# Two GELUs and three half projections at the end of attention, in a transformer layer on one core

## The chip, the cores and the metric

The kernel runs on one core of a Trainium2 chip. The metric is the device time of one execution in microseconds, as the median of several runs. Lower is better. The core has TensorE (PE, matrix products and transposes), VectorE (DVE), ScalarE (ACT), GpSimd (POOL) and SyncE (SP, which issues the transfers). Each engine takes its own instructions in order and waits on semaphores for the others.

## The reference

One layer with two groups of heads. All inputs are float32, the sequence has 2048 frames, the model width is 1024.

```python
h = rmsnorm(x, norm_mix_g)
proj = h @ w_in
y_ssm = s5_mixer(proj[..., :512], ...)          # scan, then gelu, then GLU:
#   y = gelu(y);  y = y * sigmoid(y @ w_glu + b_glu)
y_att = chunked_attention(q, k, v, rel_bias)    # softmax over 9 chunks of 64 frames
mixed = concat([rmsnorm(y_ssm, norm_ssm_out_g), rmsnorm(y_att, norm_att_out_g)])
x = x + mixed @ w_out
h2 = rmsnorm(x, norm_ffn_g)
x = x + (silu(h2 @ w_gate) * (h2 @ w_up)) @ w_down
return rmsnorm(x, norm_final_g)
```

## The kernel before

Products are made in float32 halves: an operand is cast to a high part (`gh`, `woh`, `pth`; line 153 or 884, ScalarE) and VectorE takes the rest (`gl`, `wol`, `ptl`; line 153 or 885); `mm3` then issues three products for one. Time is cut into four blocks of 512 frames (`sb`).

The program runs in stages: the input projection, attention together with the state-space scan, the mixing stage (`mix_phase`), gate and up, down. Attention goes in 128 steps, each of 128 queries of one head: `scores(s)`, then two steps later `transp(s - 2)`, which transposes the probabilities on PE into `pt` (one buffer) and casts them to `pth` and `ptl`, and after each fourth step `pv_head`, the product with the values (`pj`). Every step `s` also advances the other units. From step 119 on one of these units is the first part of the mixing stage: `mix_phase` is a generator of which `MIX_N` pieces are taken within attention, spread over steps 122 to 129, and the rest behind it.

The pieces are: fetch `yr` (the scan's output for blocks 0 and 1, four transfers) and the gate weights (`load_wg`, through the two buffers `sg`); the GELU of block 0 (`load(0, True)`, line 1050) and its casts `gh`, `gl`; the gate products of block 0 (`glu`, sixteen groups of three products into `pf`); the GELU of block 1 (`load(1, True)`). Behind attention come the gate products of block 1 (into `big`, four buffers), the split of the output weights `w_out` (`split_wo`), and the output projection. In `glu` with `late=True` the sums go back into `yr` (line 1077), and one sigmoid for all four (line 1079) and four products (line 1081) follow.

The output projection `w_out(sb, b, i)` makes two of eight row groups (a pair) in one `big` buffer. It is a generator with two halves: 24 products with the attention operands, then 24 with those of the state-space group. In block 0 two pairs are held: the first half of pair 0 is issued, then the spread of the second norm's factor `no` over partitions (four transposes `big<-ident,no`, `spread`), then the scaling `rstd2` and the cast `mixed(b, 1)` of the state-space operands, then the first half of pair 1.

The scheduler reorders ScalarE, VectorE and SP by its own estimate of readiness; the PE order is pinned to the order of the code (`keep_in_program_order`). A table of functions is loaded on ScalarE (`ACT_TABLE_LOAD`) whenever the next function is not in the one that is loaded; exponential, GELU and sigmoid are in different ones here.

Of the kernel before, what the change touches and what calls it, by code (L numbers as in the profile page):

```python
# [93 lines left out]
def f32(ap):  # L94
    return ap.bitcast(F32)
# [24 lines left out]
def spread(k, te, pb, o, c):  # L120

    for i in range(4):
        te.transpose(pb[:, i * P : (i + 1) * P], o[:, c + i : c + i + 1].to_broadcast([P, P]), k.ident[:])
# [21 lines left out]
def mm3(te, out, whi, wlo, xhi, xlo, first, last, **kw):  # L145
    te.matmul(out, whi, xhi, start=first, stop=False, **kw)
    te.matmul(out, whi, xlo, start=False, stop=False, **kw)
    te.matmul(out, wlo, xhi, start=False, stop=last, **kw)


def split(k, hi, lo, raw):
    nc = k.nc
    return nc.scalar.copy(hi, raw), nc.vector.tensor_tensor(lo, raw, f32(hi), op=ALU.subtract)  # L153
# [533 lines left out]
def att_phase(k, ident, S, aw, x0, roots):  # L687

    tc, nc, io, pfs = k.tc, k.nc, k.io, k.pfs
    with ExitStack() as cx:  # L690
# [181 lines left out]
        def transp(st):  # L872
            sb, pr, hh, qp = st
            hd = st_head[sb, 2 * pr + hh]
            if qp == 0:
                hd.p = k.t(aa, "pth", [P, 5, 4, P], F32R), k.t(aa, "ptl", [P, 5, 4, P], F32R)
            pth, ptl = hd.p
            s, k0 = hd.s.pop(qp)
            pt = k.t(psum, "pt", [P, 5, P], bufs=1)
            for kb in range(k0, qp + 5):  # L880
                k.ta.transpose(pt[:, kb % 5, :], s[:, (kb - k0) * P : (kb - k0 + 1) * P], ident[:])
            runs = [(0, 5)] if sb else ([(4, 5)] if qp == 0 else [(4, 5), (0, qp)])
            for a, b in runs:
                nc.scalar.copy(pth[:, a:b, qp, :], pt[:, a:b, :])  # L884
                nc.vector.tensor_tensor(ptl[:, a:b, qp, :], pt[:, a:b, :], f32(pth[:, a:b, qp, :]), op=ALU.subtract)  # L885

        def pv_head(st):
# [72 lines left out]
        for s in range(N + LAG + 2):  # L960
            if s == OPEN:
                aw.release()
                mix = mix_phase(k, S, lambda: k.t(pfs, "pf", [P, 512]))
                units += [Unit(islice(mix, MIX_N), MIX_N, GSTART, N + LAG, GSTART - OPEN)]
            if s == GSTART:
# [13 lines left out]
        yield mix  # L979


PY, PZ = 8, 1
MIX_N = 17 + PY + PZ


def mix_phase(k, S, bank):

    tc, nc, io = k.tc, k.nc, k.io
    te = k.te
    with ExitStack() as cx:  # L990
# [44 lines left out]
        def fetch(sb):  # L1035
            yrs[0] = k.t(my, "yr", [P, 4, L, 128])
            for f in range(4):
                nc.sync.dma_start(yrs[0][:, f], S["y"][:, f * P : (f + 1) * P, sb * 64 : sb * 64 + 128].rearrange("j p t -> p j t"))

        def load(sb, one=False):  # L1040
            b = B()
            b.o = {}
            yt = k.t(my, "ys", [P, 4, SB], bufs=2)
            b.ys, b.g = [yt[:, f] for f in range(4)], []
            if sb and sb % 2 == 0:
                fetch(sb)
            yv = b.yr = yrs[0][:, :, :, (sb % 2) * 64 : (sb % 2 + 1) * 64]
            fs = [slice(0, 4)] if one else [slice(f, f + 1) for f in range(4)]
            for s in fs:
                nc.scalar.activation(yt[:, s].rearrange("p f (c j) -> p f c j", j=L), yv[:, s].rearrange("p f j c -> p f c j"), AF.Gelu_apprx_tanh)  # L1050
            for f in range(4):
                gh, gl = k.t(my, f"gh{f}", [P, SB], F32R), k.t(my, f"gl{f}", [P, SB], F32R)
                split(k, gh[:], gl[:], b.ys[f])
                b.g.append((gh, gl))
            return b

        def load_a(b, sb):
            b.ya = [k.t(mw, f"ya{f}", [P, SB])[:] for f in range(4)]
            for f in range(4):
                nc.sync.dma_start(b.ya[f], S["ya"][sb, f * P : (f + 1) * P])  # L1060
            b.sqa = squares(b.ya)
# [33 lines left out]
        def rstd2(b, c, pb):  # L1095

            for f, (y, g) in enumerate(zip((b.ya, b.ys)[c], (ga, gs)[c : c + 1] * 4)):
                nc.vector.scalar_tensor_tensor(y, y, g[:, f : f + 1], pb, op0=ALU.mult, op1=ALU.mult)

        def big():  # L1100
            return k.t(psum, *BIG)
# [10 lines left out]
        def mixed(b, c):  # L1112
            for n, (q, y) in enumerate(zip(QS[4 * c : 4 * c + 4], (b.ya, b.ys)[c])):
                mt = k.t(mx, f"m{q}", [P, 2, SB], F32R)
                mh, ml = b.m[q] = mt[:, 0], mt[:, 1]
                split(k, mh, ml, y)

        def w_out(sb, b, i):
            ts = slice(sb * SB, (sb + 1) * SB)
            if i == 0:  # L1120
                b.sa = k.t(k.mf, "sa", [P, SB], bufs=2)
            rows = slice(i * P, (i + 2) * P)
            xt = k.t(wr, "xt", [P, 1024], bufs=2)
            xv = xt[:].rearrange("p (q t) -> p q t", q=2)
            nc.sync.dma_start(xv, io["xt"][rows, ts].rearrange("(q p) t -> p q t", p=P))
            ps = k.t(psum, *BIG)
            for n, c in ((n, c) for m in range(2) for c in range(2) for n in range(4 * m, 4 * m + 4)):
                if n == 4 and c == 0:
                    yield
                fc = slice((i + c) * P, (i + c + 1) * P)  # L1130
                for q in QS[n : n + 1]:
                    mm3(te, ps[:, c * 512 : (c + 1) * 512], W[q][0][:, fc], W[q][1][:, fc], b.m[q][0], b.m[q][1], n == 0, n == 7)
            nc.vector.tensor_tensor(xt[:], xt[:], ps[:], op=ALU.add)
            nc.sync.dma_start(S["x1"][rows, ts].rearrange("(q p) t -> p q t", p=P), xv)
            if i == 0:
                nc.scalar.activation(b.sa[:], xt[:, :512], AF.Square)
                nc.scalar.activation(xt[:, 512:], xt[:, 512:], AF.Square)
            else:
                nc.scalar.activation(xt[:], xt[:], AF.Square)
                nc.vector.tensor_tensor(b.sa[:], b.sa[:], xt[:, :512], op=ALU.add)  # L1140
            nc.vector.tensor_tensor(b.sa[:], b.sa[:], xt[:, 512:], op=ALU.add)
            yield

        def next_block(sb):
            b = load(sb)
            load_a(b, sb)
            for _ in glu(b, big):
                pass
            return b
# [12 lines left out]
        yield  # L1162
        mw = rx.enter_context(tc.tile_pool(name="mw", reuse_waits="tile", bufs=2, side="right"))
        wr = rx.enter_context(tc.tile_pool(name="wr", reuse_waits="tile", bufs=2, side="right"))
        b = load(0, True)
        load_a(b, 0)
        raws = [load_wo(n, wr, "xt") for n in range(2)]
        for _ in range(PY):
# [1 line left out]
        for n, _ in enumerate(glu(b, bank, True)):  # L1170
# [4 lines left out]
                spread(k, te, pb, b.o[0], 0)  # L1175
                rstd2(b, 0, pb[:])
            yield
        nxt = load(1, True)
        for _ in range(PZ):
            yield  # L1180

        def bk():
            nonlocal psum
# [14 lines left out]
        for sb in range(NSB):  # L1198
            if sb:
                b.m = {}  # L1200
                mixed(b, 0)
            if sb == 0:
                held = [w_out(0, b, 2 * n) for n in range(2)]
                next(held[0])
                ps = big()
                spread(k, te, ps[:, :512], b.o[1], 0)
                with tc.high_priority():
                    rstd2(b, 1, ps[:, :512])
                    mixed(b, 1)
                next(held[1])  # L1210
            else:
                mixed(b, 1)
            for n in range(4):
                if n == 0 and 0 < sb < NSB - 1:
                    nxt = next_block(sb + 1)
                if sb or n > 1:
                    for _ in w_out(sb, b, 2 * n):
                        pass
                else:
                    next(held[n])  # L1220
                if n in (0, 1) and xr:
                    next(xr)
                if n in (1, 2) and sb + 1 < NSB:
                    norm(nxt, n - 1)
                for _ in range(PRE0.get((sb, n), 0)):
                    next(pre)
                if (sb, n) == (NSB - 1, 1):
                    rx.close()
                    k.ga1 = tc.alloc_tile_pool(name="ga1", reuse_waits="tile", bufs=1, side="right")
                    k.gr = tc.alloc_tile_pool(name="gr", reuse_waits="tile", bufs=2, side="right")  # L1230
                    wr = cx.enter_context(tc.tile_pool(name="wr2", reuse_waits="tile", bufs=2, side="right"))
                    k.hT = build(k, S, 0, k.ga1, EARLY)
            if sb < NSB - 1:
                xr = rstd_steps(k, te, psum, k.mf, BIG, b.sa[:], D, S["rsn"][:, sb * SB : (sb + 1) * SB])
            if sb == 1:
                pre = pre_steps(k, S, 0, pre_tiles().__next__, True)
            k.last = b.sa[:]
            b = nxt
# [498 lines left out]
```

## Time and profile before

| | us |
|---|---|
| median of 3 runs | 2264.51 |
| lowest, highest | 2261.2, 2265.51 |
| profiled execution, its own time | 2267.91 |
| its span, first to last instruction | 2266.1 |
| PE busy | 2165.6 (96%) |
| VectorE busy | 1542.4 (68%) |
| ScalarE busy | 1003.3 (44%) |
| granted TensorE clock, mean | 0.982 |

Times in the views are microseconds from the start of the span. A bracket behind a row gives the idle time of the engine ahead of it and the instruction that ended it. The stretch that the change touches lies between 664 and 790, where attention ends and the mixing stage begins.

### The profile page before, as it was taken

Reading aid. Unit: us, or ns where it says so; the run is one execution under the profiler, and the core shown is the slowest. Engines: PE = TensorE matmul, PEld = TensorE weight load, DVE = VectorE, ACT = ScalarE, POOL = GpSimd, SP = SyncE. Lnnn points to the kernel's source line nnn. Section 1 sums busy time; section 2 is a strip of 40 time slices with the busy share of each in tenths; the row PEclk is TensorE's granted clock in tenths of the full one; section 3 lists DMA queues with packets and bytes.
Section 4 is the critical chain, followed back from the end, with each engine's and each line's share of the span. In section 5 each row is a group of like instructions: output and inputs, shape, how many; then the busy total and the mean of one; then the engine's idle time right before and its main releaser. Section 6 shows DMA issues by size and latency. Waiting matters only on the chain.

```text
span 2266.1 us, 30134 instructions
## 1 busy us (share of the span) xinstructions
PE 2165.6 (96%) x10632; PEld 1825.8 (81%) x10632; DVE 1542.4 (68%) x2695; ACT 1003.3 (44%) x1656; POOL 351.2 (15%) x827
## 2 busy tenths in 40 slices
PE   8988899999997899999999999999999999999997
PEld 6777788898986788778888887888888778888886
DVE  7756666556557756776766668766656477688776
ACT  5445555556557442353333335333333443353322
POOL 2246576656500000000000000000000010000000
PEclk9999999999998899999999999999999999999999
DMA  8878876666552435754556457645433395465652
GB/s 276 254 244 261 268 233 207 192 190 205 187 168 100 138 109 188 251 168 144 180 176 209 162 198 269 199 163 190 140 97 112 102 385 182 167 227 181 216 183 75
DMA packets 194903, 430.41 MB, mean 190 GB/s; under 512 B 19904, under 2 KB 38384, under 8 KB 187648
## 3 DMA queue, kind: packets, MB, share of 16 engines
q1 hardware_dynamic: 187104, 403.58, 53.8%
q0 software_dynamic: 7648, 24.92, 3.6%
q8 instruction: 83, 1.36, 0.2%
q14 instruction: 68, 0.56, 0.1%
HBM read 288.95 MB, written 131.10 MB: 185 GB/s over the span
## 4 chain that ended last, share of the span: by engine, by line
PE 78%; DMA 7%; DVE 6%; ACT 3%; issue 2%; SPq 0%; DVEq 0%; ACTq 0%
PE X L76 20%; PE ps L76 17%; PE Y L76 10%; PE pf L76 10%; PE big L76 6%; PE W L76 5%; PE pj L76 4%; PE pt L79 2%; PE sc L76 2%; DMA acc<-x 2%; DMA lo<-hc 1%; DMA xt<-in_xt 1%; DVE lo L153 1%; DMA hc<-gh 1%; DVE ptl L885 1%
## 5 line engine op out<-in xcount | busy, mean ns | idle before, releaser
L76 PE MATMUL X<-hi,c 128*128 128x512 f32 x1408 | 450.8, 391 | 7.4 <-DVE c L153 5.1
L76 PE MATMUL ps<-hd,hd 128*128 128x512 f32 (+1 forms) x1968 | 429.6, 380 | 3.0 <-DVE hd L153 2.0
L76 PEld LDWEIGHTS ps<-hd,hd 128*128 128x128 f32 x1968 | 357.5, 189 | 73.6 <-DVE hd L153 2.7
L76 PEld LDWEIGHTS X<-hi,c 128*128 128x128 f32 x1408 | 265.1, 188 | 64.1 <-DVE c L153 6.0
L76 PE MATMUL X<-lo,c 128*128 128x512 f32 x704 | 274.6, 390 | 0.0
L153 ACT CAST hd<-hd 128x1536 fp32r<-128x1536 f32 (+1 forms) x106 | 147.5, 1394 | 232.5 <-DMA hd<-hq 170.9
L76 PE MATMUL Y<-hi,c 128*128 128x512 f32 x704 | 226.0, 392 | 3.8 <-DVE c L153 2.3
L153 DVE TENSOR_TENSOR hd<-hd 128x1536 fp32r<-128x1536 f32 (+1 forms) x106 | 174.1, 1644 | 36.2 <-ACT hd L153 35.8
L153 DVE TENSOR_TENSOR c<-S,c 128x512 fp32r<-128x512 f32 x176 | 121.0, 688 | 103.6 <-ACT c L153 103.3
L1516 POOL DMA_DIRECT2D hd<-hq x7 | 5.3, 755 | 1173.2 <-PE X L76 1161.5
L1408 ACT COPY u<-X 128x512 f32<-128x512 f32 x132 | 77.4, 587 | 199.9 <-PE X L76 199.9
L153 ACT CAST c<-S 128x512 fp32r<-128x512 f32 x176 | 109.5, 622 | 122.5 <-PE Y L76 63.8
L76 PE MATMUL big<-m,woh 128*128 128x512 f32 x512 | 162.6, 399 | 0.0
L76 PEld LDWEIGHTS Y<-hi,c 128*128 128x128 f32 x704 | 133.3, 189 | 32.4 <-DVE c L153 2.8
L1550 DVE TENSOR_TENSOR acc<-acc,ps 128x512 f32<-128x512 f32 x196 | 130.2, 682 | 41.6 <-PE ps L76 41.3
L76 PEld LDWEIGHTS X<-lo,c 128*128 128x128 f32 x704 | 132.6, 188 | 27.4
L76 PE MATMUL pf<-hi,w 128*128 128x512 f32 x416 | 149.1, 410 | 0.0
L153 ACT CAST c<-raw 128x512 fp32r<-128x512 f32 x132 | 82.2, 622 | 149.1 <-PE Y L76 69.1
L76 PE MATMUL Y<-lo,c 128*128 128x512 f32 x352 | 137.7, 391 | 0.0
L885 DVE TENSOR_TENSOR ptl<-pt,pth 128x640 fp32r<-128x640 f32 (+3 forms) x152 | 98.3, 647 | 56.1 <-ACT pth L884 54.7
L869 ACT ACTIVATE s<-s,mn 128x640 f32<-128x640 f32 (+4 forms) x128 | 98.0, 765 | 64.1 <-DVE mn L866 58.1
L884 ACT CAST pth<-pt 128x640 fp32r<-128x640 f32 (+3 forms) x152 | 83.8, 551 | 85.6 <-PE pt L79 80.9
(448 smaller groups left out, 4274.1 us busy)
## 6 DMA issues: line engine op xcount, KB each, us to landing
w<-wss SPq DMA_DIRECT2D x36, 1024.0 KB, 6.2
hq<-g SPq DMA_DIRECT2D x140, 256.0 KB, 2.1
hd<-hq SPq DMA_DIRECT2D x35, 768.0 KB, 4.4
hd<-wc SPq DMA_DIRECT2D x35, 768.0 KB, 6.0
raw<-in_w_gate SPq DMA_DIRECT2D x44, 512.0 KB, 3.7
raw<-in_w_up SPq DMA_DIRECT2D x44, 512.0 KB, 4.2
wc<-px SPq DMA_DIRECT2D x66, 256.0 KB, 3.1
wss<-w SPq DMA_DIRECT2D x12, 1024.0 KB, 6.5
```

The source lines that it names most:

```text
L76: return self.tc.keep_in_program_order(self.tc.nc.tensor.matmul(*a, **b))
L79: return self.tc.keep_in_program_order(self.tc.nc.tensor.transpose(*a, **b))
L153: return nc.scalar.copy(hi, raw), nc.vector.tensor_tensor(lo, raw, f32(hi), op=ALU.subtract)
L869: nc.scalar.activation(s[:, :nk], s[:, :nk], AF.Exp, bias=mn[:], scale=-1.0, accum_out=sums[sb, pr][:, hh, qp : qp + 1])
L884: nc.scalar.copy(pth[:, a:b, qp, :], pt[:, a:b, :])
L885: nc.vector.tensor_tensor(ptl[:, a:b, qp, :], pt[:, a:b, :], f32(pth[:, a:b, qp, :]), op=ALU.subtract)
L1408: nc.scalar.copy(u[:], ps[:])
L1516: (nc.gpsimd if aside else nc.sync).dma_start(f32(lo), src.rearrange("g p c -> p g c"))
L1550: V.tensor_tensor(a, a, ps[:], op=ALU.add)
```

## The change

Four things are edited. `transp` keeps its last cast `pth` in `k.pth`. `load` makes the GELU in one piece only for block 1, and there `issue_after` queues it behind the last cast of probabilities; for all other blocks, block 0 among them, it is made in four pieces. One piece of `mix_phase` that only let time pass (`PZ`) is gone, so 25 pieces instead of 26 are spread over the last steps. And three pairs of the output projection are held instead of two, with the first halves of two of them ahead of the spread and that of the third behind it.

```diff
             for a, b in runs:
-                nc.scalar.copy(pth[:, a:b, qp, :], pt[:, a:b, :])
+                k.pth = nc.scalar.copy(pth[:, a:b, qp, :], pt[:, a:b, :]).ins
...
-PY, PZ = 8, 1
-MIX_N = 17 + PY + PZ
+PY = 8
+MIX_N = 17 + PY
...
-        def load(sb, one=False):
+        def load(sb):
...
-            fs = [slice(0, 4)] if one else [slice(f, f + 1) for f in range(4)]
-            for s in fs:
+            def gelu(s):
                 nc.scalar.activation(yt[:, s].rearrange("p f (c j) -> p f c j", j=L), yv[:, s].rearrange("p f j c -> p f c j"), AF.Gelu_apprx_tanh)
+
+            if sb == 1:
+                with tc.issue_after(k.pth):
+                    gelu(slice(0, 4))
+            else:
+                for f in range(4):
+                    gelu(slice(f, f + 1))
...
-        b = load(0, True)
+        b = load(0)
...
-        nxt = load(1, True)
-        for _ in range(PZ):
-            yield
+        nxt = load(1)
...
             if sb == 0:
-                held = [w_out(0, b, 2 * n) for n in range(2)]
+                held = [w_out(0, b, 2 * n) for n in range(3)]
                 next(held[0])
+                next(held[1])
                 ps = big()
                 spread(k, te, ps[:, :512], b.o[1], 0)
                 with tc.high_priority():
                     rstd2(b, 1, ps[:, :512])
                     mixed(b, 1)
-                next(held[1])
+                next(held[2])
...
-                if sb or n > 1:
+                if sb or n > 2:
                     for _ in w_out(sb, b, 2 * n):
```

Beside the edits the scheduler moves ScalarE's instructions. ScalarE before, at the first GELU (`ys_8026`): the cast of step 119 (`pth_7857`) and two exponentials (`s`) stand ahead of it, two weight casts, the copy `yt` and the cast of step 120 (`pth_8010`) behind it.

```order
L884 CAST pth_7857<-pt_7966 128x5x128
L869 ACTIVATE s_7962,sm_7946<-s_7962,mn_7963 128x640
L869 ACTIVATE s_7982,sm_7946<-s_7982,mn_7983 128x640
L1050 ACT_TABLE_LOAD
L1050 ACTIVATE ys_8026<-yr_7910 128x2048
L153 CAST wgh_1710_7915<-sg_7917 128x512
L153 CAST wgh_1713_7921<-sg_7923 128x512
L908 COPY yt_8007<-pj_7990 64x512
L884 CAST pth_8010<-pt_8012 128x5x128
```

ScalarE after, at the same place; the first row follows the copy `rb`.

```order
L1049 ACT_TABLE_LOAD
L1049 ACTIVATE ys_8026<-yr_7910 128x512
L869 ACT_TABLE_LOAD
L869 ACTIVATE s_7962,sm_7946<-s_7962,mn_7963 128x640
L884 CAST pth_7857<-pt_7966 128x5x128
L153 CAST wgh_1710_7915<-sg_7917 128x512
L869 ACTIVATE s_7982,sm_7946<-s_7982,mn_7983 128x640
L153 CAST wgh_1713_7921<-sg_7923 128x512
L1049 ACT_TABLE_LOAD
L1049 ACTIVATE ys_8026<-yr_7910 128x512 x3
L908 COPY yt_8007<-pj_7990 64x512
L153 CAST wgh_1716_7927<-sg_7929 128x512
```

One quarter of the GELU with its table has moved ahead of the exponential and the cast of step 119, and the exponential's table is loaded again behind it; the other three quarters stand behind the second exponential, and all four weight casts ahead of the cast of step 120. The window has one table load more than before.

ScalarE before, at the second GELU (`ys_8302`): behind the exponential of step 124, ahead of the casts of steps 122 and 123.

```order
L884 CAST pth_8010<-pt_8083 128x5x128
L869 ACTIVATE s_8096,sm_7946<-s_8096,mn_8097 128x640
L1050 ACT_TABLE_LOAD
L1050 ACTIVATE ys_8302<-yr_7910 128x2048
L884 CAST pth_8010<-pt_8100 128x5x128
L884 CAST pth_8010<-pt_8124 128x5x128
L869 ACT_TABLE_LOAD
L869 ACTIVATE s_8120,sm_7946<-s_8120,mn_8121 128x640
```

ScalarE after, at the second GELU (`ys_8351`): the second row is the cast of step 127.

```order
L884 CAST pth_8195<-pt_8243 128x5x128
L884 CAST pth_8195<-pt_8271 128x5x128
L1049 ACT_TABLE_LOAD
L1049 ACTIVATE ys_8351<-yr_7910 128x2048
L153 CAST gh_1808_8353<-ys_8351 128x512
L1085 ACT_TABLE_LOAD
L1085 ACTIVATE yr_7910<-yr_7910 128x32x64
L908 COPY yt_8315<-pj_8298 64x512
L153 CAST gh_1810_8357<-ys_8351 128x512
L1023 ACTIVATE sq_8340<-ys_8026 128x512
L1026 ACTIVATE sg_8342<-ys_8026 128x512
L1026 ACTIVATE sg_8345<-ys_8026 128x512
```

The second GELU has moved behind the last cast, and three of its four casts `gh` behind the load and the sigmoid of block 0 (`yr`).

PE before, around the spread in block 0 (`big_8539` is pair 0, `big_8587` pair 1, `m_1833` to `m_1836` are the attention operands):

```order
L76 MATMUL big_8539<-m_1835_8475,wol_1842_8490 128x512
L76 MATMUL big_8539<-m_1836_8478,woh_1843_8493 128x512 x2
L76 MATMUL big_8539<-m_1836_8478,wol_1844_8494 128x512
L79 MATMUL big_8564<-ident_80,no_8423 128x128 x4
L76 MATMUL big_8587<-m_1833_8469,woh_1837_8481 128x512 x2
L76 MATMUL big_8587<-m_1833_8469,wol_1838_8482 128x512
```

PE after (`big_8542` is pair 0, `big_8569` pair 1, `big_8617` pair 2):

```order
L76 MATMUL big_8569<-m_1835_8478,wol_1842_8493 128x512
L76 MATMUL big_8569<-m_1836_8481,woh_1843_8496 128x512 x2
L76 MATMUL big_8569<-m_1836_8481,wol_1844_8497 128x512
L79 MATMUL big_8594<-ident_80,no_8426 128x128 x4
L76 MATMUL big_8617<-m_1833_8472,woh_1837_8484 128x512 x2
L76 MATMUL big_8617<-m_1833_8472,wol_1838_8485 128x512
```

The 24 products of pair 1 now stand ahead of the spread, those of pair 2 behind it; before, pair 1 stood behind it and pair 2 followed later as a whole.

## The prediction

> **What bounds the kernel now.** TensorE is busy for 96% of the span, so the change can only matter where it is not. I read the busy time by stretches first, over the end of attention and the start of the mixing stage (columns: stretch, its length, then PE, PEld, DVE, ACT and POOL busy, granted clock, DMA share, GB/s).
>
> ```profile
> 676.00:690.00 14.00, 3.65 (x20) 3.02 (x18) 9.75 (x17) 13.91 (x20) 0.00 (x0) 0.71 0.64 212
> 690.00:705.00 15.00, 11.55 (x61) 10.17 (x62) 7.36 (x24) 11.03 (x13) 0.00 (x0) 0.81 0.01 1
> 720.00:735.00 15.00, 14.94 (x69) 11.73 (x67) 14.94 (x22) 11.09 (x15) 0.00 (x0) 1.00 0.61 211
> 735.00:750.00 15.00, 7.07 (x25) 5.59 (x24) 14.42 (x32) 11.44 (x17) 0.00 (x0) 0.67 0.76 235
> 750.00:800.00 50.00, 49.74 (x224) 41.19 (x224) 28.73 (x66) 23.70 (x31) 0.00 (x0) 0.96 0.35 114
> ```
>
> There are two holes. At 676 to 690 ScalarE is full (13.91 of 14.00), at 720 to 750 VectorE is. From 750 on TensorE has no room: what is won or lost before 750 stays until the end. The timeline of PE shows the waits (start, length, instruction, in brackets the idle time before it and who ended it).
>
> ```profile
> 683.69 1.30 PE L79 MATMUL pt<-ident,s 128*128 128x128 f32 x5 [6.41 <-DVE ptl L885]
> 691.81 1.30 PE L79 MATMUL pt<-ident,s 128*128 128x128 f32 x5 [5.76 <-DVE ptl L885]
> 693.33 0.63 PE L76 MATMUL pf<-gl,wgh 128*128 128x512 f32 x1
> 697.91 0.77 PE L79 MATMUL pt<-ident,s 128*128 128x128 f32 x5 [1.64 <-DVE ptl L885]
> 698.75 0.40 PE L76 MATMUL pf<-gl,wgh 128*128 128x512 f32 x1
> 713.91 0.71 PE L79 MATMUL pt<-ident,s 128*128 128x128 f32 x5
> 745.83 1.09 PE L79 MATMUL big<-ident,no 128*128 128x128 f32 x4 [7.93 <-DVE no L110]
> 753.85 0.62 PE L76 MATMUL big<-m,woh 128*128 128x512 f32 x2
> 754.53 0.62 PE L76 MATMUL big<-m,woh 128*128 128x512 f32 x2
> 767.47 0.63 PE L76 MATMUL big<-m,wol 128*128 128x512 f32 x1
> ```
>
> The transposes of probabilities (`pt`) have one PSUM buffer, so each waits until the one before was cast (`pth`, ScalarE) and its rest taken (`ptl`, VectorE). After an idle stretch the same 128x512 product takes 0.63 instead of 0.40 us: the wait of 5.76 us is followed by some 3.7 us at about half clock. The rows at 753.85 and 754.53 give the full rate: three products in 0.68 us. The row at 767.47 is slow again, with no wait ahead of it: it follows the small sums of the next block. What the casts wait for stands on ScalarE:
>
> ```profile
> 670.79 0.60 ACT L897 COPY rb<-rs 128x512 f32<-128x512 f32 x1
> 671.54 0.69 ACT L884 CAST pth<-pt 128x640 fp32r<-128x640 f32 x1 [0.15 <-PE pt L79]
> 672.13 0.83 ACT L869 ACTIVATE s<-s,mn 128x640 f32<-128x640 f32 x1
> 675.15 1.28 ACT L1050 ACT_TABLE_LOAD   x1 [0.30 <-DMA yr<-y]
> 676.45 3.69 ACT L1050 ACTIVATE ys<-yr 128x2048 f32<-128x2048 f32 x1
> 681.80 0.69 ACT L884 CAST pth<-pt 128x640 fp32r<-128x640 f32 x1
> 682.38 2.18 ACT L153 CAST gh<-ys 128x512 fp32r<-128x512 f32 x4
> 689.83 0.67 ACT L884 CAST pth<-pt 128x640 fp32r<-128x640 f32 x1
> 692.62 3.80 ACT L1050 ACTIVATE ys<-yr 128x2048 f32<-128x2048 f32 x1
> 696.33 0.68 ACT L884 CAST pth<-pt 128x640 fp32r<-128x640 f32 x1
> 714.66 0.70 ACT L884 CAST pth<-pt 128x640 fp32r<-128x640 f32 x1
> 717.99 1.92 ACT L1079 ACTIVATE yr<-yr 128x2048 f32<-128x2048 f32 x1
> 752.16 4.20 ACT L1050 ACTIVATE ys<-yr 128x512 f32<-128x512 f32 x4 [0.49 <-DVE m L153]
> ```
>
> The first GELU (676.45) holds up the cast at 681.80, the second (692.62) the one at 696.33. I name casts by step: 119 (671.54), 120 (681.80), 121, 122 (696.33), up to 127 (714.66).
>
> **The first GELU in four.** It has more to pay than before: the scheduler put one quarter ahead of cast 119, between two table loads, so there is one pair of loads more there. From 671.4, the end of `rb`: load 1.3 (1.28 and what follows 0.02 later), quarter 1.05 (a fourth of 4.20), load 1.3, exponential 0.82, and 0.1 because a load waits for the end of what is ahead. Cast 119 starts at 675.9, 4.4 us late; the products with it wait as long on PE. Then the cast 0.6, two weight casts and an exponential 1.9, load 1.4, three quarters 3.1, the copy 0.6 and two more weight casts 1.0: cast 120 at 684.6, 2.8 late. Whether data is there for this:
>
> ```profile
> yr<-y SPq DMA_DIRECT2D x1, 512.0 KB, 4.8
> DMA to landing us min/median/max: 4.8/5.9/7.2
> sg<-in_w_glu SPq DMA_DIRECT2D x4, 256.0 KB, 3.9
> xt<-in_w_out SPq DMA_DIRECT2D x2, 512.0 KB, 5.5
> ```
>
> The first quarter of `yr` is issued at 665.4 and lands 4.8 later, at 670.2, ahead of the 672.7 at which the quarter can start; the last lands, 7.2 after its issue, just before the load at 675.15. If the quarter waited for all four it would start 2.4 late, which is the upper bound. The third and fourth weight piece (`sg`) wait on SP for the rests of the first two (678) and must land by 683.6: 5.5 just does, 7.2 would cost 1 to 2.
>
> After cast 120: four casts 2.1 and three squares 1.6 put cast 121 at 688.9. Its rest stands on VectorE behind four rests of `gh`, three additions, a score step and a scaling:
>
> ```profile
> 682.72 0.82 DVE L885 TENSOR_TENSOR ptl<-pt,pth 128x640 fp32r<-128x640 f32 x1
> 690.84 0.82 DVE L885 TENSOR_TENSOR ptl<-pt,pth 128x640 fp32r<-128x640 f32 x1
> 717.45 2.49 DVE L153 TENSOR_TENSOR gl<-ys,gh 128x512 fp32r<-128x512 f32 x4
> 719.94 2.50 DVE L1081 TENSOR_TENSOR ys<-ys,yr 128x512 f32<-128x512 f32 x4
> 725.60 1.89 DVE L153 TENSOR_TENSOR m<-ya,m 128x512 fp32r<-128x512 f32 x3
> 745.53 0.16 DVE L110 SCALAR_TENSOR_TENSOR no<-nf,ny 128x4 f32<-128x4 f32 x1
> 767.02 0.16 DVE L102 TENSOR_SCALAR nv<-big 128x4 f32<-128x4 f32 x1
> 770.99 0.28 DVE L110 SCALAR_TENSOR_TENSOR no<-nf,ny 128x4 f32<-128x4 f32 x2
> ```
>
> At 0.62 each (2.49 for four) from 686.0 that is 691.8, against 690.84. PE's waits by this: 4.3 for cast 119 (672.4 to 676.7), 3.2 for the rest of 120, 2.7 for the score step behind the additions, 1.5 for the rest of 121. So the transposes of step 122 come at 692.6 instead of 691.81: **0.8 us lost**.
>
> **The second GELU behind cast 127.** Here the gain is. From the transposes of 122 to those of 123 took 6.1 us (691.81 to 697.91) with GELU and load in between. Without them: transposes at half clock 1.2, cast and rest 1.6, on PE beside them three gate products and a score step at half clock; 3.2 us, so 695.8, **2.1 us early**. From there to the transposes of 127 took 16.0 us (697.91 to 713.91); the order still has twelve groups of three gate products there and the same scores and transposes, so 16.0 stays, and cast 127 is at 712.6 instead of 714.66.
>
> But the GELU now stands in the open. After 712.6: cast 0.7, load 1.3, GELU 3.8, first `gh` cast 0.6, its rest 0.7: the first gate product of block 1 at 719.7. Then ScalarE does the load and the sigmoid of block 0 first (1.3, 1.92, to 722.2), and VectorE, in order, four products (2.5), two additions, two steps on `ya` (2.4) and only then the second rest (0.6): 727.7. **PE waits there 7.4 us**, a wait that was not there, and starts at half clock again: 2.0. The other 45 gate products take 10.2, the small sums 0.9 (an estimate from the four `ident` products at 745.83, 1.09 at half clock, for eight at full): 740.8.
>
> **Three halves ahead.** This hides it. The attention half of a pair is 24 products, 24 x 0.2275 = 5.5 us. Before, one stood ahead of the spread of `no` (745.83) and PE waited 7.93 for it. Now two do: 740.8 + 10.9 = 751.7. When is `no` there? VectorE ran without a gap from 725.60 to 745.7; it gets to the `m` rests 3.9 later (three additions and rests more, 729.5), and waits 1.1 for the second sigmoid, which needs the last gate product (741): 750.7. So PE is just the later one and waits no more. After the spread the third half runs at full clock to 757.7, by when the second operands are cast (spread plus 4.4, about 756). Before, the second halves began at 753.85 with two halves done; with a third it would have been 753.85 + 5.46 = 759.3. **The sum is 1.6 to 1.7 us gained.**
>
> Later, the sums of block 1 have 24 products instead of 48 behind them before their spread: 5.5 + 1.7 (slow after the small sums) against the 4.2 from 767.02 to 771.3: hidden, with 3 to spare; without that room each us would be paid. At most 0.3 is added because the second sums wait longer for VectorE. On SP the third `xt` load moves behind the second store, to about 769; it lands 5.5 later and is needed near 777.
>
> In the profiled execution (span 2266.1, 2267.9 with what lies around it) this is 2266.3; the median of the runs shown is 3.4 below that execution, so 2264.5 - 1.7 = **2262.8**.
>
> **Bounds.** If the clock never fell in the new waits, 727.7 would be 727.1 and PE be bound by `no`: 3.7 gained. With half-clock stretches of 4.3 us, as after 745.83, 1.2. If the last two `w_out` pieces, issued about 3.4 us later, land 2 us later than 5.5, the second sigmoid and `no` follow: 1.2 less.
>
> [...]
>
> **Rivals.** *Clock kept (faster).* The new waits do not slow PE, while the slow stretches behind 691.81 and 745.83 go: 3.7 by the bound above. The slow stretch around 767.47 comes without a wait and so hangs on where the small sums fall; they now stand behind 24 products more, and if it goes too, about twelve products at 0.2 less each, 1.7 more: 5.4 gained, 2259.1. For it: no slow row after the 1.64 us wait, and half the new waits are short. Against: 7.4 us is longer than the 5.76 after which rows are slow.
>
> *ScalarE's queue waits for transfers (slower).* ScalarE is in order and full, so a late transfer ahead of cast 119 or 120 delays all behind it, us for us: the quarter if it has to wait for the whole of `yr` 2.4; then the fourth weight piece, issued near 682 in that case, if it takes the slowest landing shown, 7.2, is there at 689.2 instead of 687.0: 2.2; then the last `w_out` pieces 1.2, and longer half-clock stretches 0.5. That is 6.3 against the 1.7 gained: 2269.1. It decides from a cast 120 later than 686.3. For it: the weight pieces queue behind four transfers of 512 KB. Against: 4.8 measured for the first quarter.
>
> *The stalls only change place (no change).* That is the sum: 13.8 us of waits in stage one before (6.41, 5.76, 1.64), 11.7 now, and 7.4 in place of 7.93.
>
> **How the numbers follow.** About 0.2% (4.5 us) is what a measurement of this kernel tells from no change. Sum 0.42 (own range 2260 to 2264.5; 0.35 within, 0.05 faster, 0.02 slower by what the runs scatter); clock kept 0.40 (0.32 faster, 0.08 within); ScalarE's queue 0.18 (0.15 slower, 0.03 within). Faster 0.37, same 0.46, slower 0.17. The range takes in both rivals and 3 us below the faster one, since the bounds on the clock are the loosest: 2256 to 2269.5.
>
> **What would show it.** Right: cast 127 about 2 us earlier; a PE wait of some 7 us in the first gate group of block 1, ended by a rest `gl`; none left ahead of the spread of `no`; three halves before the second ones. Wrong: cast 120 later than 686, a spread that still waits, or the second gate group without a wait.

## The result, and the profile after

| | before | changed |
|---|---|---|
| median of 22 runs each, us | 2264.52 | 2259.89 |
| lowest, highest | 2259.11, 2270.68 | 2255.38, 2264.78 |
| ratio, 95% interval | | 0.9979, 0.9970 to 0.9987 |
| second comparison: median (26 and 12 runs) | 2263.97 | 2261.89 |
| ratio, 95% interval | | 0.9990, 0.9980 to 0.9999 |
| profiled execution | 2267.91 | 2263.45 |
| its span | 2266.1 | 2261.7 |

The changed kernel is faster, by 4.8 us in the first comparison (ratio times the time before; 2.9 to 6.8) and by 2.3 in the second (0.2 to 4.5). The forecast was a gain of 1.7 us and 2262.8.

In the changed kernel's profile this region begins 2.88 us earlier, because the copy `rb`, up to which both programs are the same, came at 667.91 instead of 670.79. So I count from `rb`. The same stretches as those shown of before, which lie 2.88 us later in the program here (columns as in the prediction):

```profile
676.00:690.00 14.00, 6.39 (x35) 5.34 (x33) 9.63 (x17) 13.42 (x20) 0.00 (x0) 0.74 0.52 168
690.00:705.00 15.00, 15.00 (x80) 13.60 (x81) 8.87 (x27) 5.54 (x11) 0.00 (x0) 0.84 0.01 2
720.00:735.00 15.00, 8.94 (x25) 6.70 (x26) 13.61 (x21) 13.52 (x19) 0.00 (x0) 0.66 0.51 167
735.00:750.00 15.00, 15.00 (x71) 12.53 (x70) 13.73 (x31) 7.49 (x10) 0.00 (x0) 1.00 0.59 191
750.00:800.00 50.00, 49.40 (x233) 41.19 (x232) 34.27 (x76) 30.79 (x40) 0.00 (x0) 1.00 0.44 140
```

The hole at 735 to 750 (7.07 us busy before) is closed, and a hole at 720 to 735 has opened (8.94). At 690 to 705 TensorE is busy throughout, but at a granted clock of 0.84. ScalarE around the second GELU, in the timeline of the changed kernel:

```profile
667.91 0.60 ACT L897 COPY rb<-rs 128x512 f32<-128x512 f32 x1
...
711.28 0.70 ACT L884 CAST pth<-pt 128x640 fp32r<-128x640 f32 x1 [2.80 <-PE pt L79]
712.00 1.28 ACT L1049 ACT_TABLE_LOAD   x1
713.29 3.87 ACT L1049 ACTIVATE ys<-yr 128x2048 f32<-128x2048 f32 x1
717.19 0.62 ACT L153 CAST gh<-ys 128x512 fp32r<-128x512 f32 x1
717.82 1.28 ACT L1085 ACT_TABLE_LOAD   x1
719.12 1.91 ACT L1085 ACTIVATE yr<-yr 128x2048 f32<-128x2048 f32 x1
721.54 0.62 ACT L153 CAST gh<-ys 128x512 fp32r<-128x512 f32 x1
```

The GELU begins behind cast 127, as forecast, and the second `gh` stands behind the sigmoid. What waits for it, on PE (in brackets the idle time ahead of a row and who ended it):

```profile
673.77 0.50 PE L76 MATMUL pj<-pth,v 128*128 128x512 f32 x1 [4.09 <-ACT pth L884]
683.60 0.77 PE L79 MATMUL pt<-ident,s 128*128 128x128 f32 x5 [3.44 <-DVE ptl L885]
687.35 0.64 PE L76 MATMUL sc<-k,q2h 128*128 128x320 f32 x1 [2.98 <-DVE mn L866]
689.98 1.30 PE L79 MATMUL pt<-ident,s 128*128 128x128 f32 x5 [1.19 <-DVE ptl L885]
693.42 1.27 PE L79 MATMUL pt<-ident,s 128*128 128x128 f32 x5
...
717.86 0.49 PE L76 MATMUL big<-gh,wgh 128*128 128x512 f32 x1 [0.62 <-ACT gh L153]
722.21 0.79 PE L76 MATMUL big<-gh,wgh 128*128 128x512 f32 x1 [2.89 <-ACT gh L153]
726.85 0.80 PE L76 MATMUL big<-gl,wgh 128*128 128x512 f32 x1 [3.85 <-DVE gl L153]
...
751.38 0.60 PE L79 MATMUL big<-ident,no 128*128 128x128 f32 x4
769.71 1.05 PE L76 MATMUL big<-ones,sq 128*128 128x1 f32 x8 [0.60 <-DVE nv L102]
776.16 1.04 PE L79 MATMUL big<-ident,no 128*128 128x128 f32 x8
```

The three waits of the first gate group add up to 7.4 us, the last one ended by a rest `gl`; the spread at 751.38 waits for nothing. The last row is the spread of the next block's two norms. Ahead of it the same number of products has been issued in both kernels, so the time from `rb` to it is what the change did here: 108.25 us (776.16 - 667.91), against 108.67 before (779.46 - 670.79). That is 0.4 us, far less than the median shows. The experiments had to settle whether the one profile of before was typical, and which edit did what. (The empty piece `PZ` was never taken out by itself; it went with the second GELU.)

### The profile page after: what moved, and what is told of

It reads as the page before. It is cut to its first block, busy times and chain, and to the rows that moved or that the text cites. A ratio compares the mean times of both kernels' runs of the same rounds, so it can differ in the third digit from the quotient of the medians.

```text
span 2261.7 us, 30132 instructions
## 1 busy us (share of the span) xinstructions
PE 2166.7 (96%) x10632; PEld 1827.9 (81%) x10632; DVE 1541.5 (68%) x2695; ACT 1005.6 (44%) x1660; POOL 351.4 (16%) x827
## 4 chain that ended last, share of the span: by engine, by line
PE 80%; DVE 6%; DMA 5%; ACT 3%; issue 2%; SPq 0%; DVEq 0%; POOL 0%; ACTq 0%
PE X L76 20%; PE ps L76 18%; PE Y L76 10%; PE pf L76 10%; PE big L76 7%; PE W L76 5%; PE pj L76 4%; PE pt L79 2%; PE sc L76 2%; DMA lo<-hc 1%; DMA hd<-wc 1%; DMA x<-xt 1%; DVE lo L153 1%; DVE ptl L885 1%; DMA Bst<-bsts 0%
## 5 line engine op out<-in xcount | busy, mean ns | idle before, releaser
L76 PEld LDWEIGHTS ps<-hd,hd 128*128 128x128 f32 x1968 | 357.6, 189 | 75.4 <-issue 3.1
L153 ACT CAST c<-S 128x512 fp32r<-128x512 f32 x176 | 109.4, 622 | 119.7 <-PE Y L76 61.6
L76 PEld LDWEIGHTS X<-lo,c 128*128 128x128 f32 x704 | 132.9, 189 | 27.6
```

Source lines behind the costliest of these rows:

```text
L76: return self.tc.keep_in_program_order(self.tc.nc.tensor.matmul(*a, **b))
```

## The experiments

Times are medians; "ratio" is that to the kernel before in the same comparison; R is the time from `rb` to the next block's spread in the profile.

### The kernel before, twice more

No edit.

> The kernel before, unchanged, for a second profile. The stretch from `rb` to the next block's spread took 108.67 us in its first one, and 108.25 and 108.09 in the two of the changed kernel. If the sum was right in its gain, this stretch is 109.8 or more here, and the first profile was a lucky one; if the sum was wrong and the gain of the median lies elsewhere or is smaller, it is 108.7 again, within 0.7.

> The same once more, a third profile: 109.8 or more by the sum, 108.0 to 109.4 if the change gains half a microsecond or nothing in this stretch. The copy `rb` itself came at 670.79 in the first profile and between 665.9 and 668.9 in nine others with the same code ahead of it; by scatter alone it comes at 666 to 669 here.

Counted from `rb`, all five profiles and the prediction:

| | cast 127 | first product of `w_out` | spread of `no` | next block's spread (R) |
|---|---|---|---|---|
| before, three profiles | 43.9, 44.3, 46.8 | 61.0, 61.4, 64.0 | 75.0, 75.4, 77.8 | 108.7, 106.6, 111.4 |
| predicted | 41.8 | 70.0 | 80.9 | 107.0 |
| changed, two profiles | 43.4, 43.2 | 72.6, 72.4 | 83.5, 83.3 | 108.3, 108.1 |

The second profile (2261.46 us) lies below both expectations, the third (2265.06) agrees with the sum: the scatter of one kernel is larger than what was to be told apart. `rb` came at 668.25 and 666.23, so the late one of the first profile was scatter. The spread of 4.8 us in R goes with the clock: the waits add up to 23 us in each, and half clock between `rb` and the next block's spread to 23.9, 27.3 and 30.7 us where R is 106.6, 108.7 and 111.4. In the windows view of the third profile of before:

```profile
690.00:705.00 15.00, 13.15 (x61) 11.46 (x60) 7.05 (x23) 7.39 (x10) 0.00 (x0) 0.76 0.00 1
```

TensorE was busy 13.15 of 15 us there, at 0.76 of the clock. The trace's clock record has half clock from 10.5 to 24.2 and again from 27.6 to 34.4 after `rb`, where the first profile has it, up to cast 127, from 11.2 to 24.9 alone. On means the change wins 0.7 us in R (108.9 to 108.2).

### The changed kernel once more

No edit.

> The changed kernel once more, for a second profile of it. The stretch from the copy `rb` at the end of step 119's group to the spread of the next block's two norms took 108.67 us before and 108.25 in the changed kernel's profile. Theory of the sum, with the gain where it was put: that stretch is again within 2 us of 108.25, and what else the median has is scatter of the rest of the program, which both kernels share. Rival, that the first profile of the changed kernel was an unlucky one in this stretch: 105 us or less here, by half-clock stretches that fall otherwise.

2261.89, ratio 0.9990 (0.9980 to 0.9999), R 108.09. The first profile was no unlucky one.

### Three halves alone

```diff
-                held = [w_out(0, b, 2 * n) for n in range(2)]
+                held = [w_out(0, b, 2 * n) for n in range(3)]
                 next(held[0])
+                next(held[1])
...
-                next(held[1])
+                next(held[2])
...
-                if sb or n > 1:
+                if sb or n > 2:
```

> The kernel before with three held pairs alone; both GELUs stay as they were. Theory of the sum: `no` is ready at the same time (745.7), TensorE has 5.5 us more work ahead of it, so its wait ahead of the spread falls from 7.93 to about 2.4 and the second halves begin 5.5 earlier; if the short wait leaves the clock at full, 2 more. 5.5 to 7.5 us faster than before, 2257 to 2259. By this theory the two other edits of the change together cost some 1 to 3 us. Rival, that the gain of the change comes from the second GELU and the third half only covers for it: less than 2 us faster, 2262.5 to 2264.5, since `no` comes when it came.

2258.71, ratio 0.9975 (0.9962 to 0.9988): 5.6 us faster (2.7 to 8.6); R 105.5. On PE, the spread of `no` in this kernel:

```profile
746.12 0.86 PE L79 MATMUL big<-ident,no 128*128 128x128 f32 x4 [2.71 <-DVE no L110]
```

The wait is 2.71 in place of 7.93. The rival is out: the third half gains by itself, and by its median as much as the whole change (on another chip, and the intervals overlap). From the first product of `w_out` to the next block's spread it takes 42.3 us, where before took 47.6, 45.2 and 47.4. The half clock was not saved (3.4 us of it follow the spread), so the gain is the lower end of what was expected.

### The second GELU behind the last cast, alone

```diff
-                nc.scalar.copy(pth[:, a:b, qp, :], pt[:, a:b, :])
+                k.pth = nc.scalar.copy(pth[:, a:b, qp, :], pt[:, a:b, :]).ins
...
-PY, PZ = 8, 1
-MIX_N = 17 + PY + PZ
+PY = 8
+MIX_N = 17 + PY
...
             for s in fs:
+              with tc.issue_after(k.pth) if sb == 1 else ExitStack():
```

> The kernel before with the second GELU behind the last cast (and the empty piece gone), two held pairs, the first GELU whole. Theory of the sum: cast 127 some 2 us earlier, then 7 us of waits in the first gate groups of block 1 and a `no` about 5 later, with only one half (5.5 us) in front of it: the wait ahead of the spread stays at 4 to 5 us, and the time is 3 to 5 us longer than before, 2267.5 to 2269.5. Rival, that the edit gains by itself: 1 to 2 us faster than before, 2262.5 to 2263.5.

2266.82, ratio 1.0008 (0.9997 to 1.0020), R 114.8. On PE:

```profile
719.54 0.79 PE L76 MATMUL big<-gh,wgh 128*128 128x512 f32 x1 [2.89 <-ACT gh L153]
724.18 0.79 PE L76 MATMUL big<-gl,wgh 128*128 128x512 f32 x1 [3.85 <-DVE gl L153]
747.33 1.09 PE L79 MATMUL big<-ident,no 128*128 128x128 f32 x4 [4.08 <-DVE no L110]
```

Cast 127 came 41.8 after `rb`, some 2 us earlier than in the first two profiles of before, as forecast. The waits of the changed kernel are there (2.89, 3.85), and without a third half 4.08 remain ahead of the spread, as the sum has it. By the times this edit gains nothing: its interval leaves out any gain over 0.7 us; whether it costs 2 or 4.5 they don't tell. The profile's R says 6 more than the mean of before.

### The first GELU in four, alone, and undone

```diff
-        b = load(0, True)
+        b = load(0)
```

> The kernel before with the first GELU in four alone. ScalarE's order shows that the second GELU then stands right behind the casts of the first, without a table load of its own. Theory of the sum: cast 119 4.4 late, cast 121 about where it was, 0.8 lost at the transposes of step 122, then the second GELU ends about 3 earlier than before and steps 122 and 123 follow each other without a load between: within 1.5 us of before, 2263 to 2266. Rival, that the additional pair of loads delays all that follows: 2.6 slower, 2267.

2263.06, ratio 0.9989 (0.9975 to 1.0004), R 107.0, within what before shows: no loss. Undone in the changed kernel:

```diff
-            if sb == 1:
+            if sb == 0:
+                gelu(slice(0, 4))
+            elif sb == 1:
```

> The changed kernel with the first GELU in one piece again (second GELU behind the last cast, three halves). Theory of the sum: the cast of step 122 comes some 0.8 (the term in the sum) to 1.3 us (22.09 in the kernel with the second GELU alone behind, 23.40 in the change, both from `rb`) earlier, and all up to the spread with it: 0.8 to 1.3 us faster than the changed kernel, 2258 to 2260. Rival, that the four pieces are what makes the change gain: slower than the changed kernel by 1 or more, 2261 to 2264.

2260.82, ratio 0.9984 (0.9973 to 0.9996), beside 2261.89 for the changed kernel in the same comparison (0.9980 to 0.9999): the times do not tell the two apart. R is 107.95 beside 108.09. Cast 122 came 0.9 earlier (22.28 for 23.19 from `rb`), but cast 127 only 0.4 (42.79 for 43.20). With the two long waits back, 6.35 and 5.75, half clock lasted until 27.0 after `rb`, and until 26.7 in the changed kernel; so what came earlier ran more of its work at half clock, and from cast 123 to cast 124 it took 7.3 us in place of 6.8. Of the 0.4, 0.3 went into a longer wait for `gl` (4.15 for 3.85). So the four pieces cost what the sum said at one end, and nearly all of it comes back behind them.

### The second GELU behind the last exponential

The casts of the last steps don't need the GELU's table to be out of the way, only the exponentials do: in the first profile of before the cast at 696.33 follows the GELU of 692.62 with no load between, and the next exponential (700.73) has a load of 1.28 ahead of it. So the GELU can begin behind the last exponential, in quarters between the last casts.

```diff
-            nc.scalar.activation(s[:, :nk], s[:, :nk], AF.Exp, bias=mn[:], scale=-1.0, accum_out=sums[sb, pr][:, hh, qp : qp + 1])
+            k.ex = nc.scalar.activation(s[:, :nk], s[:, :nk], AF.Exp, bias=mn[:], scale=-1.0, accum_out=sums[sb, pr][:, hh, qp : qp + 1]).ins
...
-                with tc.issue_after(k.pth):
-                    gelu(slice(0, 4))
+                with tc.issue_after(k.ex):
+                    for f in range(4):
+                        gelu(slice(f, f + 1))
```

> The changed kernel with the second GELU in four and queued behind the last exponential instead of the last cast. Theory of the sum: the waits of the attention end stay short (casts 126 and 127 at most 1 to 2 us later), the 7.6 us of waits in the first gate groups of block 1 and the half clock behind them (2.0) go, `no` comes 7 to 8 earlier and stays hidden behind two halves: 7 to 9 us faster than the changed kernel, 2251 to 2253. Rival, that the waits only move to the casts of the last steps: within 2 us of the changed kernel, 2258 to 2262.

2258.79, ratio 0.9975 (0.9961 to 0.9990), R 104.15. The waits in the gate group are gone, and the first product of `w_out` comes 61.8 after `rb` in place of 72.6. But the time is short of the 7 to 9 us expected against the changed kernel: `no` was ready at 75.9 in place of 82.1, 6.2 earlier only, and PE waits for it again. On PE the small sums and the spread, on VectorE the first and the last step of the factor:

```profile
727.48 0.94 PE L76 MATMUL big<-ones,sq 128*128 128x1 f32 x8
744.97 0.98 PE L79 MATMUL big<-ident,no 128*128 128x128 f32 x4 [2.74 <-DVE no L110]
```

```profile
733.39 0.15 DVE L102 TENSOR_SCALAR nv<-big 128x4 f32<-128x4 f32 x1
...
744.67 0.15 DVE L110 SCALAR_TENSOR_TENSOR no<-nf,ny 128x4 f32<-128x4 f32 x1
```

The sums are done at 728.4; VectorE takes them up 5 us later and needs 11.4 us for steps of 0.15 each, since a rest, an addition or a product stands between nearly any two of them. I had let `no` follow the gate products; it follows VectorE's row of work. Three variants follow (the first of them timed twice), all with the first GELU whole again:

> First GELU whole, second GELU in four behind the last exponential, three halves. Against the kernel with the first GELU in four (104.15 us from `rb` to the next block's spread): 1.3 less up to the gate products. Theory that TensorE sets the pace there: 102.8, 2257.5. Rival, that VectorE's row of work up to `no` sets it and starts no earlier: 104 to 105 with a wait of 4 us ahead of the spread, 2258.5.

2253.37, ratio 0.9954 (0.9938 to 0.9970), R 103.64; the wait ahead of the spread is 2.54. Once more on another chip:

> First GELU whole, second in four behind the last exponential, three halves, as timed before (six runs, ratio 0.9954), for the comparison with the row above on the same chip. If that ratio was not luck: 0.994 to 0.997 again, and 103 to 104.5 us from `rb` to the next block's spread. Rival, that it was luck: 0.9975 as with the first GELU in four.

2255.54, ratio 0.9974 (0.9965 to 0.9983), R 102.51. R fits the first theory better, though `no` still ends a wait of 1.95 and 2.54; the first time is lower than either theory had it. 0.9974 is what the rival had, so the size of the first ratio was in good part luck, the sign not: 6 to 10 us faster than before. In the first comparison its interval lies clear of that of the changed kernel (0.9980 to 0.9999) and of the changed kernel with the first GELU whole (0.9973 to 0.9996), which differs from it in the second GELU alone, all timed on the same chip. R agrees (103.64 and 102.51 beside 107.95), so behind the last exponential is a better place than behind the last cast. Against three halves alone (0.9975) no gain is shown: the first product of `w_out` comes 61.6 and 61.0 after `rb`, as it did before (61.0, 61.4, 64.0), since casts 126 and 127 now wait for the quarters of the GELU (with the first GELU in four, cast 126 begins at 708.52 as a quarter of 1.13 ends, and cast 127 at 713.10 behind three more of 3.09 and a cast `gh`), and from there to the next block's spread it takes 42.1 and 41.5 beside 42.3.

With the factor on GpSimd:

```diff
-                rstd1(b, 1, bk())
+                rstd1(b, 1, bk(), newton_pool)
```

> As the kernel before this one, with the factor `no` of block 0's second norm computed on the idle GpSimd (thirteen small steps and three more) instead of between VectorE's large ones. Theory that VectorE's order holds up `no`: the sums stand ready on PE at 728 and VectorE takes them up at 733.4 and is done at 744.8; on GpSimd, at 0.23 to 0.3 us a step, `no` is there 5 us after its first step, before 740, so no wait is left ahead of the spread, and the half clock behind it goes: 4 us less, 98 to 99.5 us from `rb` to the next block's spread, 2253.5 to 2254.5. Rival, that the operands behind the spread (scaling and rests on VectorE) come no earlier: the wait moves behind the third half and less than 1.5 us is gained.

2259.67, ratio 0.9980 (0.9967 to 0.9992), R 107.2: slower than without it, as neither theory had it. `newton_pool` has the same steps on GpSimd, with the first multiplication on ScalarE. On GpSimd, VectorE and PE:

```profile
733.38 0.20 POOL L121 TENSOR_SCALAR nf<-nf 128x4 f32<-128x4 f32 x1
733.65 5.86 POOL L123 TENSOR_SCALAR nv<-nv 128x4 f32<-128x4 f32 x1
740.18 0.73 POOL L125 TENSOR_TENSOR nf<-ny 128x4 f32<-128x4 f32 x1
...
744.84 0.20 POOL L125 TENSOR_TENSOR nf<-ny 128x4 f32<-128x4 f32 x1
745.71 0.20 POOL L128 TENSOR_TENSOR no<-nf,ny 128x4 f32<-128x4 f32 x1
```

```profile
734.66 2.35 DVE L171 TENSOR_TENSOR wol<-xt,woh 128x1024 fp32r<-128x1024 f32 x2
736.93 2.49 DVE L1108 TENSOR_TENSOR ys<-ys,yr 128x512 f32<-128x512 f32 x4
...
745.96 1.11 PE L79 MATMUL big<-ident,no 128*128 128x128 f32 x4 [5.41 <-POOL no L128]
```

A step of this size took 0.20 where VectorE was idle (744 to 747) and up to 5.86 where VectorE took rests and products without a pause. PE then waits 5.41 for `no`.

With the sums earlier:

```diff
-R1 = 13
+R1 = 10
```

> First GELU whole, second in four behind the last exponential, three halves, and the small sums of block 0's second norm three gate groups earlier (R1 from 13 to 10). VectorE's order shows `no` ahead of two additions and a rest that stood ahead of it. Theory that the small steps' place in VectorE's row sets `no`: it comes 1.5 to 2.5 earlier, the wait of 2.54 ahead of the spread falls under 1 and the half-clock stretch of 3.4 behind it goes: 100.5 to 102 from `rb` to the next block's spread (103.64 without this). Rival, that VectorE's whole row of work up to the operands sets the end: the wait only moves behind the third half, 103 to 104.

2253.50, ratio 0.9957 (0.9941 to 0.9972), R 103.61. On PE:

```profile
741.08 0.62 PE L79 MATMUL big<-ident,no 128*128 128x128 f32 x4 [0.90 <-DVE no L110]
747.82 0.50 PE L76 MATMUL big<-m,woh 128*128 128x512 f32 x1 [0.42 <-DVE m L153]
760.19 1.36 PE L76 MATMUL big<-ones,sq 128*128 128x1 f32 x8 [0.60 <-DVE nv L102]
766.68 1.05 PE L76 MATMUL big<-m,woh 128*128 128x512 f32 x2
```

The wait for `no` fell to 0.90 and no half clock follows the spread, as the theory had it; one wait for the operands `m` appeared, as the rival had it, but of 0.42 only. R stayed for another reason. The half clock at the next block's small sums lasted 6.8 us (94.5 to 101.3 after `rb`; the row at 766.68 is still slow) in place of 3.4, which takes back what was saved behind the spread, and the first product of `w_out` came 0.7 later (62.3 for 61.6). So neither theory is decided by this one profile, and the time, on the same chip as the second timing above (0.9974), can't be told from it either. These two are the best versions found.

## Why the prediction was right, and where not

**The number.** The sum had 1.7 us; the medians say 4.8 (2.9 to 6.8) and 2.3 (0.2 to 4.5), and R, the stretch that the sum is about, says 0.4 against the first profile of before and 0.7 on means. The median of 2259.89 lies in the stated range, but that range (2256 to 2269.5) was made to hold both rivals too, and the median lies next to the 2259.1 of the faster rival, half of which the trace refutes. The waits and what covers them were forecast rightly; that the time agrees is in part luck.

**The waits.** Cast 119 came 5.13 after `rb` (forecast 5.1), cast 120 13.9 (13.8), cast 121 18.2 (18.1). PE's waits up to there were 4.09, 3.44, 2.98 and 1.19 (forecast 4.3, 3.2, 2.7 and 1.5). The gate group's waits are 7.4 as forecast, the last one ended by `gl`; none is left ahead of the spread; three halves stand ahead of the second ones. ScalarE's transfers were in time, so the slower rival is out: cast 120 came at 684.7 in the times of before, against 686.3 from which it decides.

**Where the sum failed: "16.0 stays".** From the transposes of 123 (0.5 later than forecast) to those of 127 the changed kernel took 17.1 (693.42 to 710.54). Half clock lasted until 26.9 us after `rb`, against 24.9 in the first profile of before, so the first 1.4 us of this stretch ran at half clock, which costs 0.7; two short waits of 0.29 and 0.21, where before had one of 0.15, are nearly all the rest. Cast 127 came 1.6 later than forecast. From there to the first product of `w_out` it took 29.2 in place of 28.2: 0.5 up to the rest `gl`, and 0.5 because the half clock that begins in the waits lasted 10.2 us by the clock record, some 5.5 of it on running products. That makes `w_out` 2.6 late. Against this the slow stretch after the small sums was absent (granted clock 1.00 in 750 to 800, against 0.96): 1.7, which the sum had not counted. So 1.7 forecast, less 2.6, less 0.34 because the small sums waited 0.60 in place of 0.26, plus 1.7: 0.4, as R shows it against the first profile of before.

**The faster rival.** Its first half, that the new waits don't slow PE, is wrong (the rows of 0.79 and 0.80 at 722.21 and 726.85). Its second half came true in the profiles of the change, but the stretch is also absent in one of the three profiles of before, so it can't be put down to the change. (Its "twelve products at 0.2 less each" would be 2.4; 3.4 us at half clock hold eight such products, 0.43 us apart at 767.47 and 767.90, and its 1.7 is right.)

**The rest of the gain was not found.** From the next block's spread to the end the profiles show 0.5 us on means (1485.6 before, 1485.1 changed), which with the 0.7 of R makes 1.2: less than either median, and five single executions are too few to tell from it where the rest is. The 0.5 is made of parts that differ by more: to the end of `w_out` 176.4 to 177.4 before, 178.0 changed; gate and up stage (first product `X` to first product `ps<-hd`) 853.3, 854.5 and 854.7 before, 850.6 and 850.7 changed; from there to the end 452.3 to 454.2 before, 454.6 and 455.4 changed. The 3.5 us in the gate and up stage have two places. One is its first products; on PE, before and changed:

```profile
960.22 0.73 PE L76 MATMUL X<-hi,c 128*128 128x512 f32 x2 [1.68 <-DVE c L153]
965.57 1.22 PE L76 MATMUL Y<-hi,c 128*128 128x512 f32 x2 [2.33 <-DVE c L153]
```

```profile
956.76 0.73 PE L76 MATMUL X<-hi,c 128*128 128x512 f32 x2 [0.41 <-DVE c L153]
```

VectorE's order is the same there in both. Part of this is time that only changed its place: counted from the first of two stores `x<-xt`, for which ScalarE's row waits there, the first product comes 0.1 us later in all profiles of before, and 1.4 and 1.5 later in those of the change, so the rests that it needs are nearer. The other place is the middle of the stage, some 443 us after its first product, where PE waits about 3.4 us in both kernels; before and changed:

```profile
1403.02 1.22 PE L76 MATMUL X<-hi,c 128*128 128x512 f32 x2 [3.45 <-DVE c L153]
1407.46 0.63 PE L76 MATMUL Y<-hi,c 128*128 128x512 f32 x1
```

```profile
1397.93 1.22 PE L76 MATMUL X<-hi,c 128*128 128x512 f32 x2 [3.47 <-DVE c L153]
1401.91 0.40 PE L76 MATMUL Y<-hi,c 128*128 128x512 f32 x1
```

By the clock record the half clock at this wait lasts 6.8 us in all three profiles of before and 3.4 in both of the change, which is 1.7 us. The kernel with three halves alone has 0.41 at the first products, 3.4 of half clock in the middle and 850.5 as well; the second GELU alone has 2.00, 3.4 and 851.7, the first in four alone 1.69, 6.8 and 853.9. So the first products go with the third half rather than with the GELUs, but the kernel with earlier sums has three halves and 853.6. What causes it stays open, and no experiment was made on it.

**What each edit is worth.** The price of the second GELU behind the last cast (waits of 7.4 and half clock) and the worth of the third half (5.5) were right in kind and nearly in size: the edit alone leaves 4.08 of wait ahead of the spread and gains nothing, the half alone is 5.6 us faster. The earlier end of attention that the GELU's move was made for is there (cast 127 at 41.8, 43.4 and 43.2 against 43.9, 44.3 and 46.8), but the waits behind it take it back. With the GELU behind the last exponential those waits are gone, and no gain beyond that of the third half is shown.

## What to carry to other kernels

When two edits are made together and one covers what the other costs, time each alone: here the cover alone gained as much as both, by the medians. An instruction that has to leave a crowded stretch should be queued behind the last one that conflicts with it (the last exponential, for the table), not behind the last of the stretch; that made the changed kernel faster, though not shown to be faster than leaving the GELU where it was. And a baseline taken from a single profile carries its own luck: the same stretch of the same kernel took 106.6 to 111.4 us.

## What the runs showed of the hardware

**How long half clock lasted.** In the clock records of the first profiles of before and of the change every stretch of half clock inside the program lasts 3.41, 6.83, 10.24 or 13.65 us. Nearly the same three waits (6.41, 5.76 and 1.64; 6.27, 5.75 and 1.85) gave 13.7 us of it in one execution of the kernel before, and 13.7 and 6.8 in another. Short waits went with slow products in some profiles and not in others. Behind the wait of 1.85 in the third profile of before a 128x512 product took 0.63 us, up to 34.4 after `rb`; behind that of 1.64 in the first it took 0.40. Around the next block's small sums (eight products of 128x1) a wait of 0.26 was followed by half clock of 3.4 us in the first profile of before. A wait of 0.60 at the same place was followed by 6.8 us with the sums earlier, and by none in both profiles of the change (0.39 a product).

**GpSimd beside VectorE.** Steps of 4 columns took 0.20 to 0.22 us with VectorE idle (744 to 747), and 0.19 to 5.86 beside its rests, additions and products. The step of 5.86 us (733.65 to 739.51) lasts over two rests and four products in a row (734.66 to 739.42); what held it was not shown. (The profile's spans on GpSimd are rough; PE's wait of 5.41 for the last step agrees with them.)
